# The pooling branch's output product as seven products of quarters instead of eight

## The chip, the cores and the metric

The kernel runs on one core of a Trainium2 chip. The metric is the device time of one execution in microseconds, lower is better; each figure is the median of several runs.

## The reference

One decoder block of width 1024 over 1024 positions, in float32. After a modulated norm, one projection makes q, k, v, z_a, u, z_b, m_a and m_b. A stick-breaking attention branch and a pooling branch are gated and mixed. The pooling branch is what changes:

```python
pooled = multiscale_causal_pool(u, pool_w, pool_scale)
p_b = (pooled * jax.nn.silu(z_b)) @ w_branch_b
merged = jax.nn.sigmoid(m_a) * p_a + jax.nn.sigmoid(m_b) * p_b
out = merged @ w_out
return x + gate[:, None, :] * out
```

Here (pooled * silu(z_b)) is 1024 x 1024 and w_branch_b is 1024 x 1024.

## The kernel before

**Split products.** Every float32 operand is held as two float32r tiles, a rounded one (hi) and the rest (lo = value - hi). A product a·b is three matmuls per block, hi·hi, hi·lo and lo·hi, into one PSUM bank. One matmul has a stationary block of 128 x 128 and 512 moving columns, so an output bank of 128 x 512 over an inner size of 1024 takes 24 matmuls. load_w loads a 128-column tile of a weight into `raw` (2 buffers) and splits it into `whl` (2 buffers): a cast by one engine (L123 ACT or L127 DVE), a subtraction by another (L118, DVE or POOL).

**Stages.** In order: the modulated norm and the first half of u; the second half of u (8 banks); v (16 banks, two halves of eight); z_b (wzb, 8 tiles of two banks each); the pooling product (pb, 8 tiles of two banks); then one long stage with the remaining projections (p) woven into the attention; then the branch sums (pa) and the output (o). Positions run along the free dimension, so the pooling product takes weight blocks as stationary and `gb` as moving operand: gb[j] is channel block j of pooled * silu(z_b), 128 x 1024, held as hi and lo. Each output bank is copied by ACT (L661) into `sm` and stored to pb_d, which is read much later.

**PSUM.** Eight banks in four tags of two: pj, z, av, tr. The projections and the pooling product use pj alone. ACT reads a bank (u_sg, vo, zs or sm), in v and wzb DVE too, before PE can write it again.

**Low tiles.** The lo half of 32 weight tiles of the long stage is made ahead of time by make_lo and kept in HBM (wl_d). One low tile: SP loads the tile (l_raw, L152), ACT casts it (l_hi, L155), DVE subtracts in place (L156), SP stores it (wl_d, L157). Eight are placed in u, ten in v, four in wzb, ten in pb (LO_V, LO_ZB, LO_PB). They are first read in the long stage, after its eighth weight tile.

**Order.** Outside the hand-pinned parts a scheduler decides, when the program is built, in which order each engine takes its instructions; on the chip each engine's queue and the DMA queues of SP and ACT are strictly in order, so an instruction that waits holds all behind it on its engine. A tile's buffer count (bufs) says how many uses may overlap.

Of the kernel before, what the change touches and what calls it, by code (L numbers as in the profile page):

```python
# [9 lines left out]
F32 = mybir.dt.float32  # L10
F32R = mybir.dt.float32r
# [46 lines left out]
def block_kernel(ctx, tc, a, out):  # L58
# [3 lines left out]
    def pool(name, **kw):  # L62
        return tc.tile_pool(name=name, bufs=1, reuse_waits="tile", **kw)
# [9 lines left out]
    def bank(tag, name):  # L73
        return psp.tile([P, 512], F32, tag=tag, bufs=BANKS[tag], name=name)
# [64 lines left out]
    tiles += gates  # L139
    early_lo = iter(range(PLAIN, len(tiles)))  # L140

    def make_lo(pl, n, tag=None, bufs=3, later=False):

        rest = []
        for _ in range(n):
            i = next(early_lo)
            if tag:
                raw, hi = (pl.tile([P, D], t_, tag=tag, bufs=5, name=f"l{i}_{n_}") for n_, t_ in (("raw", F32), ("hi", F32R)))
            else:
                raw = pl.tile([P, D], F32, tag="lraw", bufs=bufs, name=f"l{i}_raw")  # L150
                hi = pl.tile([P, D], F32R, tag="lhi", bufs=1, name=f"l{i}_hi")
            nc.sync.dma_start(raw, a["w_in"][tiles[i]])  # L152

            def low(i=i, raw=raw, hi=hi):
                act.copy(hi, raw)  # L155
                v.tensor_sub(raw.bitcast(F32R), raw, hi.bitcast(F32))  # L156
# [31 lines left out]
    def hmov(sh):  # L188
        return lambda m, kb: m[:, kb, sh * 512:sh * 512 + 512]
# [390 lines left out]
    with pool("vp") as vp:  # L580
        def load_wv(hf, k2):
            raw = wts.tile([P, 2, 512], F32, tag="raw", bufs=2, name=f"wv{hf}_{k2}_raw")
            nc.sync.dma_start(raw.rearrange("p k c -> p (k c)"), a["w_v"][hf, k2])
            return split(raw, [P, 2, 512], vp, "wv", 6, act, v, f"wv{hf}_{k2}")

        wv = [[load_wv(0, k2) for k2 in range(4)]]
        for i in reversed(range(KB)):
            ps = bank("pj", f"u{i}_1")
            mm3(ps, whl[i], h, range(KB), hmov(1))
            use[i](1, ps)  # L590
            make_lo(vp, 1)
        early.close()
        diffs = ExitStack()
        todo = []
        dif = diffs.enter_context(pool("dif", side="right"))
        for hf in range(2):
            if hf == 0:
                wv.append([load_wv(1, k2) for k2 in range(4)])
            for sb in range(8):
                ss = slice(sb * P, (sb + 1) * P)  # L600
                ps = bank("pj", f"v{sb}_{hf}")
                for kb in range(KB):
                    hh, hl = h_hi[:, kb, ss], h_lo[:, kb, ss]
# [6 lines left out]
                act.copy(vo[:, :, 0], pv)  # L610
                v.tensor_sub(vo[:, :, 1], pv, vo[:, :, 0].bitcast(F32))  # L611
# [12 lines left out]


    with pool("pb") as pb:
        gb = pb.tile([P, 2, KB, S], F32R, name="gb")
        for j in range(KB):
            if j not in dhls:
                make_d(j, load_u(j))  # L630
            zs = [pb.tile([P, 512], F32, tag="zs", bufs=3, name=f"zs{j}_{sh}") for sh in range(2)]

            def silu(sh, ps):
                z, sl = zs[sh], slice(sh * 512, sh * 512 + 512)
                act.activation(z, ps, AF.Sigmoid)
                v.tensor_mul(z, ps, z)
# [12 lines left out]
        gate = pb.tile([P, KB], F32, name="gate")
        bias = pb.tile([P, KB], F32, name="gbias")  # L650
        nc.sync.dma_start(bias, a["b_gate"])
        for j in range(KB):
            sm = [pb.tile([P, 512], F32, tag="zs", bufs=3, name=f"sm{j}_{sh}") for sh in range(2)]
            whl = load_w(a["w_branch_b"][j], f"wb{j}", v, gp)
            wg = wts.tile([P, D], F32, tag="raw", bufs=2, name=f"wg{j}")
            nc.sync.dma_start(wg, a["w_gate"][j])
            v.scalar_tensor_tensor(gjunk, wg, 1.0, sg, ALU.mult, ALU.mult, accum_out=gate[:, j:j + 1])
            for sh in range(2):
                ps = bank("pj", f"pb{j}_{sh}")
                mm3(ps, whl, (gb[:, 0], gb[:, 1]), range(KB), hmov(sh))  # L660
                act.copy(sm[sh], ps)  # L661
# [442 lines left out]
```

## Time and profile before

| | us |
|---|---|
| median of 3 runs | 1210.2 (1209.76 to 1210.31) |
| span of the profiled execution | 1210.3 |
| u, second half, and what goes before v | 91 to 128 |
| v | 128.4 to 216.5 |
| wzb | 216.7 to 303.7 |
| pb | 303.7 to 390.8 |
| long stage with p | 390.8 to about 1029 |

The profile counts an engine as busy while it has an instruction in work. For PE, matmuls overlap (one shows as 389 ns), so the rate is read from the length of an unbroken run divided by its count. "DMA share" is the mean busy share of the core's 16 DMA engines. "x<-y" names what an instruction writes and reads. A wait counts as idle time of the engine, put down to what ended it. The granted TensorE clock was 0.999 over the execution.

### The profile page before, as it was taken

How to read it: one execution, taken by the hardware profiler on the slowest of the kernel's cores; microseconds unless marked ns; L12 is line 12 of the kernel's file. 1: busy time of each engine (PE TensorE's matmuls, PEld its weight loads, DVE VectorE, ACT ScalarE, POOL GpSimd, SP SyncE). 2: the span in 40 equal slices, each digit the busy share in tenths (PEclk: the TensorE clock that was granted, in tenths of full speed). 3: DMA queues.
4: the chain of work that ended last, by engine and by line, in shares of the span. 5: the costliest groups of instructions: out<-in, count | busy, mean ns of one | idle time of the engine just before them, and what ended most of it. 6: DMA issues, size and time to landing. Idle time of an engine off the chain costs nothing.

```text
span 1210.3 us, 16177 instructions
## 1 busy us (share of the span) xinstructions
PE 1199.2 (99%) x5746; PEld 1002.5 (83%) x5746; DVE 756.5 (63%) x1050; ACT 531.6 (44%) x1008; POOL 187.2 (15%) x360
## 2 busy tenths in 40 slices
PE   8999999999999999999999999999999999999997
PEld 7888878888888888888888888888888888888886
DVE  5764483677510286767868677686777853785643
ACT  5564331334301255655555555655555643232211
POOL 1000000001221333212222222222221210000001
PEclk9999999999999999999999999999999999999999
DMA  9649995626847632442635325353343344975622
GB/s 358 255 171 325 328 356 207 209 87 225 309 148 120 191 91 76 124 122 86 170 109 156 113 80 153 110 157 118 102 134 101 99 131 167 353 272 170 216 67 83
DMA packets 81955, 207.14 MB, mean 171 GB/s; under 512 B 10449, under 2 KB 23889, under 8 KB 79698
## 3 DMA queue, kind: packets, MB, share of 16 engines
q1 hardware_dynamic: 73666, 191.23, 49.2%
q10 hardware_dynamic: 8208, 14.88, 3.3%
q8 instruction: 45, 0.74, 0.2%
q14 instruction: 36, 0.29, 0.1%
HBM read 138.96 MB, written 50.34 MB: 156 GB/s over the span
## 4 chain that ended last, share of the span: by engine, by line
PE 88%; DMA 5%; issue 3%; DVE 2%; ACT 1%; POOL 0%; POOLq 0%; ACTq 0%; DVEq 0%; SPq 0%
PE p L103 34%; PE pb L103 7%; PE wzb L103 7%; PE pa L103 7%; PE o L103 6%; PE z L103 6%; PE av L103 5%; PE wt L103 5%; PE v L103 4%; PE ua L103 3%; DMA wl_d<-l_raw 2%; DMA l_raw<-in_w_in 2%; PE u L103 2%; PE wm L103 1%; DVE l_raw L156 1%
## 5 line engine op out<-in xcount | busy, mean ns | idle before, releaser
L103 PE MATMUL p<-hT,w 128*128 128x512 f32 x1920 | 480.0, 391 | 0.5 <-ACT m_sg L201 0.5
L103 PEld LDWEIGHTS p<-hT,w 128*128 128x128 f32 x1920 | 355.2, 188 | 74.7 <-ACT m_sg L201 1.0
L826 DVE TENSOR_TENSOR_SCAN om<-om 128x512 f32<-128x512 f32 (+7 forms) x128 | 175.8, 1373 | 124.9 <-ACT om L819 69.4
L819 ACT ACTIVATE om<-z 128x512 f32<-128x512 f32 (+2 forms) x192 | 94.5, 492 | 155.9 <-PE z L103 133.5
L824 POOL TENSOR_SCALAR_AFFINE_SELECT om<-om 128x128 f32<-128x128 f32 x128 | 56.3, 440 | 346.5 <-ACT om L819 287.0
L846 DVE TENSOR_TENSOR wt<-wt,wt 128x512 fp32r<-128x512 f32 (+1 forms) x160 | 99.3, 621 | 16.1 <-ACT wt L845 15.5
L845 ACT CAST wt<-wt 128x512 fp32r<-128x512 f32 (+1 forms) x160 | 88.2, 551 | 48.1 <-PE wt L103 47.9
L103 PE MATMUL av<-wt,vv 128*128 128x512 f32 x320 | 106.4, 414 | 0.0
L103 DVE TENSOR_TENSOR be<-be,om 128x511 f32<-128x511 f32 (+7 forms) x128 | 95.1, 749 | 1.1 <-POOL be L824 0.7
L820 ACT ACTIVATE be<-z 128x512 f32<-128x512 f32 (+2 forms) x192 | 94.1, 490 | 0.0
L103 PE MATMUL pa<-ga,wa 128*128 128x512 f32 x384 | 89.6, 389 | 0.1
L103 PE MATMUL o<-wo,mhl 128*128 128x512 f32 (+1 forms) x408 | 89.6, 377 | 0.0
L103 PE MATMUL wt<-ident,be 128*128 128x128 f32 x576 | 89.4, 273 | 0.0
L103 PE MATMUL v<-wv,hT 128*128 128x512 f32 x384 | 87.8, 390 | 0.5 <-DVE vo L611 0.5
L103 PE MATMUL wzb<-hT,wzb 128*128 128x512 f32 x384 | 87.2, 389 | 0.0
L103 PE MATMUL pb<-gb,wb 128*128 128x512 f32 x384 | 87.2, 389 | 0.0
L103 PEld LDWEIGHTS v<-wv,hT 128*128 128x128 f32 x384 | 71.9, 188 | 16.2 <-DVE vo L611 1.4
L103 PEld LDWEIGHTS o<-wo,mhl 128*128 128x128 f32 x408 | 73.5, 188 | 14.1
L103 PEld LDWEIGHTS pa<-ga,wa 128*128 128x128 f32 x384 | 72.0, 188 | 15.4 <-DVE wa L118 0.5
L103 PEld LDWEIGHTS wzb<-hT,wzb 128*128 128x128 f32 x384 | 72.1, 188 | 14.9
L103 PEld LDWEIGHTS pb<-gb,wb 128*128 128x128 f32 x384 | 72.1, 188 | 14.9
L103 PEld LDWEIGHTS wt<-ident,be 128*128 128x128 f32 x576 | 70.2, 141 | 11.6
(130 smaller groups left out, 1364.5 us busy)
## 6 DMA issues: line engine op xcount, KB each, us to landing
w_raw<-in_w_in SPq DMA_DIRECT2D x40, 512.0 KB, 4.7
l_raw<-in_w_in SPq DMA_DIRECT2D x32, 512.0 KB, 5.2
wl_d<-l_raw SPq DMA_DIRECT2D x32, 512.0 KB, 5.7
w<-wl_d SPq DMA_DIRECT2D x32, 512.0 KB, 3.8
v_d<-vo SPq DMA_DIRECT2D x16, 512.0 KB, 5.2
vv<-v_d SPq DMA_DIRECT2D x8, 1024.0 KB, 5.3
wa_raw<-in_w_branch_a SPq DMA_DIRECT2D x16, 512.0 KB, 4.7
wa<-in_w_mod SPq DMA_DIRECT2D x7, 1024.0 KB, 6.4
```

The source lines that it names most:

```text
L103: ins = op(*args, **kw)
L156: v.tensor_sub(raw.bitcast(F32R), raw, hi.bitcast(F32))
L819: act.activation(om[:, b0:b0 + n], zp[:, :n], AF.Sigmoid, scale=-0.125)
L820: act.activation(be[:, b0:b0 + n], zp[:, :n], AF.Sigmoid, scale=0.125)
L824: gp.affine_select(out=tl[:, :P], in_=tl[:, :P], pattern=[[1, P]], compare_op=ALU.is_gt, fill=fill, base=0, channel_multiplier=-1)
L826: v.tensor_tensor_scan(om[:, :W], om[:, :W], om[:, :W], 1.0, ALU.mult, ALU.min)
L845: act.copy(wt[:, 0, :off], pt[:, :off])
L846: v.tensor_sub(wt[:, 1, :off], pt[:, :off], wt[:, 0, :off].bitcast(F32))
```

## The change

Three edits, made together.

**1. Seven products.** With output columns (weight halves m), inner halves k and position halves n, the product of 2 x 2 quarters is made by seven products of sums and differences of quarters (the form of Strassen's method with shared sums). `gb` now holds the plain float32 value, in place of hi and lo; t1 and t2 hold differences of its quarters, s2k sums of weight quarters. For each product and each half q of its inner size (256 rows each), the operands are loaded, combined on DVE and split (a_op for weights in the `whl` buffers, b_op for activations in `bhl`), and 4 output blocks x 2 inner blocks x 3 matmuls follow. All eight PSUM banks are used: p1, p6, p7 and p4 sum up in one set of four (pj, z), p5 and p3 in the other (av, tr), p2 in the first again. The results go out as copies (ACT) and additions (DVE).

**2. Low tiles.** ACT writes the negative of the cast (l_neg), a DMA issued by POOL adds the raw tile to it, and SP stores that. Raw and negative tiles have two buffers each; raw had three in u and v, and five shared ones in pb. The numbers placed in u, v and wzb stay, and LO_PB spreads its ten over seven products.

**3. Placement.** The vo tiles get a pool of their own. The gate's eight products with w_gate move from pb into the wzb loop and share the raw tiles' two buffers there. w_branch_b is passed untiled.

```diff
-LO_PB = (1, 1, 1, 1, 1, 1, 2, 2)
+LO_PB = (1, 2, 1, 2, 1, 2, 1)
...
-    def make_lo(pl, n, tag=None, bufs=3, later=False):
+    def make_lo(pl, n, bufs=2, later=False):
...
+            raw = pl.tile([P, D], F32, tag="lraw", bufs=bufs, name=f"l{i}_raw")
+            neg = pl.tile([P, D], F32R, tag="lneg", bufs=2, name=f"l{i}_neg")
             nc.sync.dma_start(raw, a["w_in"][tiles[i]])
 
-            def low(i=i, raw=raw, hi=hi):
-                act.copy(hi, raw)
-                v.tensor_sub(raw.bitcast(F32R), raw, hi.bitcast(F32))
-                nc.sync.dma_start(wl_d[i], raw)
+            def low(i=i, raw=raw, neg=neg):
+                act.mul(neg, raw, -1.0)
+                gp.dma_start(neg.bitcast(F32), raw, accum_op=ALU.add)
+                nc.sync.dma_start(wl_d[i], neg.bitcast(F32))
...
-                vo = dif.tile([P, 8, 2, HD], F32R, tag="vo", bufs=3, name=f"vo{sb}_{hf}")
+                vo = vop.tile([P, 8, 2, HD], F32R, tag="vo", bufs=3, name=f"vo{sb}_{hf}")
...
-        gb = pb.tile([P, 2, KB, S], F32R, name="gb")
+    gb = pb.tile([P, KB, S], F32, name="gb")
+    t1 = pb.tile([P, 4, 512], F32, name="t1")
+    t2 = pb.tile([P, 4, 512], F32, name="t2")
...
+    def b_op(src, name):
+        hl = pb.tile([P, 2, 2, 512], F32R, tag="bhl", bufs=3, name=name)
+        act.copy(hl[:, 0], src)
+        v.tensor_sub(hl[:, 1], src, hl[:, 0].bitcast(F32))
+        return hl
...
+    def a_op(src, name):
+        hl = wts.tile([P, 2, 2, 512], F32R, tag="whl", bufs=2, name=name)
+        act.copy(hl[:, 0], src)
+        v.tensor_sub(hl[:, 1], src, hl[:, 0].bitcast(F32))
+        return hl
...
+        if j < 4:
+            v.tensor_sub(t1[:, j], gb[:, j, 512:], gb[:, j, :512])
+        else:
+            v.tensor_sub(t2[:, j - 4], gb[:, j, 512:], t1[:, j - 4])
+            v.tensor_sub(gb[:, j - 4, 512:], gb[:, j, 512:], gb[:, j - 4, 512:])
+        make_lo(pb, LO_ZB[j])
...
+        wg = pb.tile([P, D], F32, tag="lraw", bufs=2, name=f"wg{j}")
...
-            whl = load_w(a["w_branch_b"][j], f"wb{j}", v, gp)
...
-            for sh in range(2):
-                ps = bank("pj", f"pb{j}_{sh}")
-                mm3(ps, whl, (gb[:, 0], gb[:, 1]), range(KB), hmov(sh))
-                act.copy(sm[sh], ps)
-                nc.sync.dma_start(pb_d[j][:, sh * 512:sh * 512 + 512], sm[sh])
-            make_lo(dif, LO_PB[j], "d")
...
+    def a_s1(q):
+        r, w = raw1(1, 0, q, f"a21_{q}"), raw2(1, 1, q, f"a22_{q}")
+        v.tensor_add(r, r, w)
+        w = raw2(0, 0, q, f"a11s_{q}")
+        v.tensor_sub(k2(s2k, q), r, w)
+        return r
...
+    products = (
+        ("p1", lambda q: raw1(0, 0, q, f"a11_{q}"), lambda q: part(gb, 0, 0, q)),
+        ("p5", a_s1, lambda q: k2(t1, q)),
+        ("p6", lambda q: k2(s2k, q), lambda q: k2(t2, q)),
+        ("p7", a_s3, lambda q: part(gb, 0, 1, q)),
+        ("p4", lambda q: raw1(1, 1, q, f"a22_{q}"), b_t4),
+        ("p3", a_s4, lambda q: part(gb, 1, 1, q)),
+        ("p2", lambda q: raw1(0, 1, q, f"a12_{q}"), lambda q: part(gb, 1, 0, q)),
+    )
+    ta, tb = ("pj", "pj", "z", "z"), ("av", "av", "tr", "tr")
...
+        for q in range(2):
+            wl_, ml_ = a_op(a_of(q), f"{name}a{q}"), b_op(b_of(q), f"{name}b{q}")
+            for j in range(4):
+                for e in range(2):
+                    for i, (w, m) in enumerate(((0, 0), (0, 1), (1, 0))):
+                        mm(
+                            ps[j], wl_[:, w, e, j * P:(j + 1) * P], ml_[:, m, e],
...
+            elif name == "p7":
+                out_b(j + 4, 1, added(copied("s3", 2, j, ps[j]), chain["b"][j]))
+            elif name == "p4":
+                out_b(j + 4, 0, copied("s4", 2, j, ps[j]))
...
+        make_lo(pb, LO_PB[n])
```

The changed program's order is known before it runs. On PE, before, the pooling product is a plain row of banks, 24 matmuls each, tile by tile (the name is the bank, then the operands):

```order
L103 MATMUL wzb_1_2306<-hT,wzb_2273 128x512 x24
L103 MATMUL pb_0_2360<-gb,wb_2354 128x512 x24
L103 MATMUL pb_1_2387<-gb,wb_2354 128x512 x24
L103 MATMUL pb_0_2430<-gb,wb_2424 128x512 x24
L103 MATMUL pb_1_2457<-gb,wb_2424 128x512 x24
```

Now, at the passage from the second half of product p7 to p4 (p7a and p7b are its weight and activation operands, 2639 and 2642 those of the second half; p_0 to p_3 are the four banks):

```order
L103 MATMUL p_0_2351<-p7b_2642,p7a_2639 128x512 x4
L103 MATMUL p_1_2352<-p7b_2642,p7a_2639 128x512 x4
L103 MATMUL p_2_2353<-p7b_2642,p7a_2639 128x512 x4
L103 MATMUL p_3_2354<-p7b_2642,p7a_2639 128x512 x4
L103 MATMUL p_0_2351<-p4b_2703,p4a_2699 128x512 x6
L103 MATMUL p_1_2352<-p4b_2703,p4a_2699 128x512 x6
L103 MATMUL p_0_2351<-p4b_2736,p4a_2732 128x512 x2
L103 MATMUL p_1_2352<-p4b_2736,p4a_2732 128x512 x2
L103 MATMUL p_0_2351<-p4b_2736,p4a_2732 128x512 x4
L103 MATMUL p_1_2352<-p4b_2736,p4a_2732 128x512 x4
L103 MATMUL p_2_2353<-p4b_2703,p4a_2699 128x512 x6
```

The banks are now woven: p4 takes the second half of its operands (p4a_2732) after 12 matmuls on the first half, two banks at a time.

On ACT, at the passage from u to v, before (l_hi is the cast of a low tile; nine such casts stand ahead of the first vo here, of which these rows show the last three):

```order
L155 CAST l_hi<-l_raw 128x1024
L208 COPY u_sg_1082<-u_1_1057 128x512
L209 DMA u_d<-u_sg_1082 128x512
L155 CAST l_hi<-l_raw 128x1024
L208 COPY u_sg_1116<-u_1_1091 128x512
L155 CAST l_hi<-l_raw 128x1024
L209 DMA u_d<-u_sg_1116 128x512
L610 CAST vo_0_1174<-v_0_1149 128x8x64
L155 CAST l_hi<-l_raw 128x1024 x2
L610 CAST vo_0_1206<-v_0_1181 128x8x64
```

And now (l_neg is the negation of a low tile; the one just ahead of vo_0_1177 is the seventh):

```order
L152 ACTIVATE l_neg<-l_raw 128x1024
L205 COPY u_sg_1116<-u_1_1091 128x512
L206 DMA u_d<-u_sg_1116 128x512
L152 ACTIVATE l_neg<-l_raw 128x1024
L609 CAST vo_0_1177<-v_0_1152 128x8x64
L152 ACTIVATE l_neg<-l_raw 128x1024
L609 CAST vo_0_1209<-v_0_1184 128x8x64
L609 CAST vo_0_1244<-v_0_1219 128x8x64
L152 ACTIVATE l_neg<-l_raw 128x1024
L609 CAST vo_0_1283<-v_0_1258 128x8x64
```

Two low tiles have moved from u into v, and in v they stand further apart; sixteen stores of low tiles now stand ahead of the last v_d store in SP's queue, before it was eighteen.

On ACT again, at the end of wzb, before (zs and gb belong to the wzb banks):

```order
L635 ACTIVATE zs_0_2186<-wzb_0_2193 128x512
L155 CAST l_hi<-l_raw 128x1024
L638 CAST gb<-zs_0_2186 128x512
L155 CAST l_hi<-l_raw 128x1024
L635 ACTIVATE zs_1_2187<-wzb_1_2223 128x512
L638 CAST gb<-zs_1_2187 128x512
L635 ACTIVATE zs_0_2269<-wzb_0_2276 128x512
L155 CAST l_hi<-l_raw 128x1024
```

And now (wzb_0_2107 is the eleventh of the sixteen banks, wzb_1_2305 the last; p1a are weight operands of the first product):

```order
L152 ACTIVATE l_neg<-l_raw 128x1024 x2
L663 ACTIVATE gb<-wzb_0_2107 128x512
L663 ACTIVATE gb<-wzb_1_2135 128x512
L123 CAST wzb_2274<-wzb_raw 128x1024
L152 ACTIVATE l_neg<-l_raw 128x1024 x2
L663 ACTIVATE gb<-wzb_0_2195 128x512
L663 ACTIVATE gb<-wzb_1_2223 128x512
L653 CAST p1a_2357<-a_0_2355 128x1024
L152 ACTIVATE l_neg<-l_raw 128x1024 x2
L663 ACTIVATE gb<-wzb_0_2277 128x512
L663 ACTIVATE gb<-wzb_1_2305 128x512
L653 CAST p1a_2389<-a_1_2387 128x1024
```

The negations now stand in pairs, one pair to two banks, and a fourth pair follows right behind these rows, ahead of the casts for p5. From the first p tile of the long stage on, the order of every engine is the old one.

More of the change, by code (lines that the diff above doesn't have):

```diff
@@ L667, in block_kernel, with part @@
-    diffs.close()
+        vouts.close()
+    pbs = ExitStack()
+    pb = pbs.enter_context(pool("pb"))
+    gb = pb.tile([P, KB, S], F32, name="gb")
+    t1 = pb.tile([P, 4, 512], F32, name="t1")
+    t2 = pb.tile([P, 4, 512], F32, name="t2")
+    gate = pb.tile([P, KB], F32, name="gate")
+    bias = pb.tile([P, KB], F32, name="gbias")
+    nc.sync.dma_start(bias, a["b_gate"])
+    sg = pb.tile([P, D], F32, name="sg")
+    def part(src, k, n, q):
+        return src[:, 4 * k + 2 * q:4 * k + 2 * q + 2, 512 * n:512 * n + 512]
@@ new lines, in b_op, with load_a @@
+    def b_op(src, name):
[3 more added lines that the diff above has]
+        return hl
+    def load_a(m, k, q, pl, tag, name):
+        raw = pl.tile([P, 2, 512], F32, tag=tag, bufs=2, name=name)
+        r0 = (4 * k + 2 * q) * P
+        nc.sync.dma_start(raw, a["w_branch_b"][r0:r0 + 2 * P, 512 * m:512 * m + 512].rearrange("(k p) c -> p k c", p=P))
+        return raw
+    def a_op(src, name):
[3 more added lines that the diff above has]
+        return hl
@@ new lines, in block_kernel, with silu @@
+    for j in range(KB):
+        if j not in dhls:
+            make_d(j, load_u(j))
+        def silu(sh, ps):
+            z = gb[:, j, sh * 512:sh * 512 + 512]
+            act.activation(z, ps, AF.Sigmoid)
+            v.tensor_mul(z, ps, z)
+            v.scalar_tensor_tensor(z, dhls[j][:, sh * 512:sh * 512 + 512], psc_v[:, j:j + 1], z, ALU.mult, ALU.mult)
+        project(CZB + j, f"wzb{j}", silu, act, v)
+        if j < 4:
[4 more added lines that the diff above has]
+        make_lo(pb, LO_ZB[j])
+        if j == 0:
+            nc.sync.dma_start(sg, a["c_row"].broadcast_to([P, D]))
+            gjunk = pb.tile([P, D], F32, tag="lraw", bufs=2, name="gjunk")
+            act.activation(gjunk, sg, AF.Sigmoid)
+            v.tensor_mul(sg, sg, gjunk)
+        wg = pb.tile([P, D], F32, tag="lraw", bufs=2, name=f"wg{j}")
+        nc.sync.dma_start(wg, a["w_gate"][j])
+        v.scalar_tensor_tensor(wg, wg, 1.0, sg, ALU.mult, ALU.mult, accum_out=gate[:, j:j + 1])
+        del dhls[j]
@@ new lines, in block_kernel, with raw1, raw2, k2 @@
+    v.tensor_add(gate, gate, bias)
+    nc.sync.dma_start(g_d[0].rearrange("(k p) -> p k", p=P), gate)
+    diffs.close()
+    sums = pbs.enter_context(pool("sums", side="right"))
+    s2k = sums.tile([P, 4, 512], F32, name="s2k")
+    def raw1(m, k, q, name):
+        return load_a(m, k, q, wts, "raw", name)
+    def raw2(m, k, q, name):
+        return load_a(m, k, q, sums, "ar", name)
+    def k2(t, q):
+        return t[:, 2 * q:2 * q + 2]
+    def a_s1(q):
[4 more added lines that the diff above has]
+        return r
@@ new lines, in block_kernel, with out_b, copied, added @@
+    ta, tb = ("pj", "pj", "z", "z"), ("av", "av", "tr", "tr")
+    chain = {}
+    keep = {}
+    def out_b(j, n, t):
+        nc.sync.dma_start(pb_d[j][:, 512 * n:512 * n + 512], t)
+    def copied(tag, bufs, j, src):
+        t = sums.tile([P, 512], F32, tag=tag, bufs=bufs, name=f"{tag}_{j}")
+        act.copy(t, src)
+        return t
+    def added(t, src):
+        v.tensor_add(t, src, t)
+        return t
+    for n, (name, a_of, b_of) in enumerate(products):
+        c = {"p5": "b", "p3": "b", "p2": "c"}.get(name, "a")
+        if c not in chain:
+            chain[c] = [bank((tb if c == "b" else ta)[j], f"{name}_{j}") for j in range(4)]
+        ps = chain[c]
+        for q in range(2):
[5 more added lines that the diff above has]
+                            ps[j], wl_[:, w, e, j * P:(j + 1) * P], ml_[:, m, e],
+                            start=name in ("p1", "p5", "p2") and (q, e, i) == (0, 0, 0), stop=(q, e, i) == (1, 1, 2),
+                                skip_group_check=True,
+                        )
+        for j in range(4):
+            if name == "p1":
+                keep["s1", j] = copied("s1", 4, j, ps[j])
+            elif name == "p6":
+                keep["s2", j] = copied("s2", 4, j, ps[j])
+            elif name == "p7":
+                out_b(j + 4, 1, added(copied("s3", 2, j, ps[j]), chain["b"][j]))
+            elif name == "p4":
+                out_b(j + 4, 0, copied("s4", 2, j, ps[j]))
+            elif name == "p3":
+                out_b(j, 1, added(keep["s2", j], ps[j]))
+            elif name == "p2":
+                out_b(j, 0, added(keep["s1", j], ps[j]))
+        make_lo(pb, LO_PB[n])
@@ L670, in block_kernel @@
+    pbs.close()
     logits = ExitStack()
```

49 lines of the change are left out of this document (14 added, 35 removed).

## The prediction

> **What bounds the kernel now.** I read the page first: busy times, then the chain that ended last.
>
> ```profile
> PE 1199.2 (99%) x5746; PEld 1002.5 (83%) x5746; DVE 756.5 (63%) x1050; ACT 531.6 (44%) x1008; POOL 187.2 (15%) x360
> PE 88%; DMA 5%; issue 3%; DVE 2%; ACT 1%; POOL 0%; POOLq 0%; ACTq 0%; DVEq 0%; SPq 0%
> ```
>
> TensorE is busy for 99% of the span and carries 88% of the chain. A busy PE need not be useful, so the next view is the chain in order of time (start, length, what):
>
> ```profile
> 216.69 87.04 PE wzb L103 x384
> 303.73 87.04 PE pb L103 x384
> 390.77 25.16 PE p L103 x111
> ```
>
> The two stages around the change, the z_b projection (wzb) and the pooling product (pb), are unbroken runs of 384 matmuls at 87.04 / 384 = 0.2267 us each. One PSUM bank of 24 matmuls takes 5.44 us. While PE runs like this, everything else is free only as long as it stays ahead. The table by stage shows how far ahead (stretch, length, then PE, PEld, DVE, ACT, POOL busy, PE clock, DMA share, GB/s):
>
> ```profile
> 91.00:128.00 37.00, 37.00 (x164) 30.31 (x163) 14.42 (x13) 15.25 (x19) 0.00 (x0) 1.00 0.90 313
> 128.00:216.50 88.50, 87.97 (x387) 72.22 (x386) 49.10 (x66) 23.54 (x31) 0.00 (x0) 1.00 0.83 293
> 216.50:303.50 87.00, 87.00 (x385) 72.07 (x384) 64.06 (x81) 33.87 (x47) 3.27 (x1) 1.00 0.51 172
> 303.50:390.60 87.10, 87.10 (x386) 72.13 (x385) 23.20 (x31) 16.04 (x23) 19.13 (x8) 1.00 0.69 197
> ```
>
> In the u and v stages (91 to 216.5) the scarce thing beside PE is the DMA engines, at 0.90 and 0.83. In wzb it is DVE, 64 of 87 us. In pb nothing is scarce. PE waited there hardly at all:
>
> ```profile
> PE v L103 <- DVE vo L611: 0.5, 2, 0.3
> ```
>
> But the low tiles already run just in time. The chain between 90 and 180 us passes through them:
>
> ```profile
> 95.41 1.06 ACT l_hi L155
> 96.49 1.24 DVE l_raw L156
> 97.74 5.66 DMA wl_d<-l_raw
> 103.47 9.17 DMA l_raw<-in_w_in
> ```
>
> Cast, subtraction, store and next load follow each other in one buffer, 17 us a turn here, with three buffers. And ACT, which must empty the PSUM banks, stands behind them:
>
> ```profile
> 124.62 1.05 ACT L155 CAST l_hi<-l_raw 128x1024 fp32r<-128x1024 f32 x1 [5.79 <-DMA l_raw<-in_w_in]
> 125.57 0.58 ACT L208 COPY u_sg<-u 128x512 f32<-128x512 f32 x1
> ```
>
> ACT idled 5.79 us for a load, and a finished bank of u waited behind it. With two banks, PE stops only if a copy is later than 5.44 - 0.59 = 4.85 us. So there is a margin, and it was partly used.
>
> **What goes: matmuls.** Eight products of quarters become seven. Each is 4 column blocks x 4 row blocks x 3 = 48 matmuls, so 384 become 336. I take the same 0.2267 us each: all have one loaded 128x128 block against 512 columns, and the wzb run, which loads as often, has that rate. 48 x 0.2267 = **-10.9 us**, all on PE and all on the chain. Nothing else in this change shortens the chain, so 1210.3 - 10.9 = 1199.4 is the floor. From the first p tile on, each engine's new order is the old one, so no term lies behind 391 us.
>
> **What comes: operand work.** Each of 28 operand halves (14 weight, 14 activation) needs a cast on ACT and a subtraction on DVE; ten more subtractions or additions of 1024 columns form the combinations, and 28 copies and additions read PSUM. The prices:
>
> ```profile
> L118 DVE TENSOR_TENSOR wzb<-wzb_raw,wzb 128x1024 fp32r<-128x1024 f32 x6 | 7.3, 1217 | 0.0
> L636 DVE TENSOR_TENSOR zs<-wzb,zs 128x512 f32<-128x512 f32 x15 | 10.3, 687 | 10.4 <-ACT zs L635 10.4
> L661 ACT COPY sm<-pb 128x512 f32<-128x512 f32 x16 | 9.4, 588 | 59.1 <-PE pb L103 59.1
> L123 ACT CAST w<-w_raw 128x1024 fp32r<-128x1024 f32 x2 | 2.1, 1052 | 0.0
> L118 POOL TENSOR_TENSOR w<-w_raw,w 128x1024 fp32r<-128x1024 f32 x2 | 4.8, 2392 | 17.8 <-ACT w L123 17.8
> ```
>
> DVE: 38 x 1.217 + 12 x 0.687 = 54.5 us. ACT: 28 x 1.052 + 16 x 0.588 = 38.9, with ten negations at 1.05 49.4. Both lie beside 336 x 0.2267 = 76.2 us of PE, and the first few are made during wzb. The worst product, p5, asks 8 x 1.217 = 9.7 us of DVE in its 10.9. So on average it is hidden, at little margin. In wzb DVE loses about 9 subtractions of low tiles (11.0) and 16 of gb (11), and gains 12 differences (8.2), six gate products (7.3) and six operand splits (7.3): 64 becomes about 65 of 87. Cost nothing, with 20 us of cover.
>
> The product stage has edges, though. A weight buffer of a block is free only when the block two before has finished, and then cast and subtraction take 1.05 + 1.22 = 2.3 us of a block's 5.44. In p4 the order lets PE reach the second block after 12 matmuls, 2.7 us, so there 0.4 us is left. At the end, the first p tile takes its buffer 5.44 us before the last product ends and needs 1.05 + 2.39 = 3.4 us: it fits. I cost these edges at **+1 us**. Below stands nothing; above, a late load at each of the last six blocks at about a microsecond, 6 us.
>
> **What is moved: the low tiles.** The subtraction leaves DVE; ACT now writes the negative cast, and a DMA from POOL's queue adds the raw tile to it. The trace has no DMA that adds. Its time X, issue to landing, has these nearest rows:
>
> ```profile
> q<-qlo SPq DMA_DIRECT2D x32, 128.0 KB, 2.4
> vv<-v_d SPq DMA_DIRECT2D x8, 1024.0 KB, 5.3
> wa<-in_w_mod SPq DMA_DIRECT2D x7, 1024.0 KB, 6.4
> wa<-in_w_mod SPq DMA_DIRECT2D x2, 512.0 KB, 10.2
> ```
>
> The lower end is 2.4 (SBUF to SBUF, a quarter of the size), the upper 10.2 (the right size, at the start, when the engines were full). The addition must fetch both tiles, 1024 KB, so I take the 1024 KB rows: 5.3 where the engines are half idle, 6.4 where they are full. The Trainium skill, "DMA: Bandwidth & Descriptors", section "Anatomy of one DMA — SWDGE (gpsimd) path", fits a DMA from this queue as 2.0 us + bytes / 436e3, which gives an estimate of 3.2 us for one tile; by it X would cost nothing anywhere and the sum would be 1200.4. No run here shows that fit yet. "Collectives: The Full Stack", section "The bandwidth ceiling: the fold count and why AG ≠ RS ≠ AR", says that an adding DMA is slow because it reads two sources, not because of the addition; that would make it 4.4 us, still under what I take.
>
> Now the turn of a buffer. The load of the tile after next waits for X, with two buffers each for raw and negative: turn = landing + negation + X. Landings:
>
> ```profile
> l_raw<-in_w_in SPq DMA_DIRECT2D x17, 512.0 KB, 6.5
> wl_d<-l_raw SPq DMA_DIRECT2D x18, 512.0 KB, 6.8
> l_raw<-in_w_in SPq DMA_DIRECT2D x10, 512.0 KB, 4.9
> ```
>
> (The first two are of 80 to 200 us, the last of 230 to 335.) The order of ACT gives the deadlines. The first negation can stand where the first cast stood, and the seventh, three turns later, stands ahead of the first vo copy:
>
> ```profile
> 90.67 1.05 ACT L155 CAST l_hi<-l_raw 128x1024 fp32r<-128x1024 f32 x1
> 133.99 0.59 ACT L610 CAST vo<-v 128x512 fp32r<-128x512 f32 x1 [2.60 <-PE v L103]
> ```
>
> It may start at 133.99 + 4.85 - 1.05 = 137.8 at the latest: three turns in 47.1, 15.7 us a turn. With the median landing a turn is 6.5 + 1.05 + 6.4 = 14.0, which fits. But the additions make the engines fuller, so I take the longest landing seen, 9.17: 16.6, which is 0.9 over in each of three turns, **+3 us** (2.8). Ends: nothing at X = 2.4; at X = 10.2, 20.4 a turn, 3 x 4.7 = 14 us.
>
> In wzb, pairs of negations stand between the ACTIVATEs that empty its banks. The first pair follows unit 10, which ends at 216.69 + 54.4 = 271.1; the fourth stands ahead of the cast for p5, needed by about 303.7 + 10.9 - 2.3 = 312. After 0.6 of ACTIVATE and 2.1 for the last pair, three turns in 38.2 us: 12.7 each. A turn costs 4.9 + 2.1 + 5.3 = 12.3: **0**, by 0.4 us. At X = 10.2 it is 17.2, 3 x 4.5 = 14 us; below, nothing. SP matters here too: its queue is in order, and behind each store of a low tile, which waits for the addition, stand v_d stores, wzb loads and the loads of p5. They slip by the same lag as ACT, not once more. On POOL the additions have only each other behind them until the first p tile; the eight subtractions of weight blocks (2.4 us and more each) are gone from it.
>
> **Sum.** 1210.3 - 10.9 + 1 + 2.8 + 0 = 1203.2 by the profiled execution, whose span is 0.1 above the median of the runs. I give **1203.3 us**.
>
> **Rivals.**
>
> 1. *The additions overfill the DMA engines in u and v, and it ends slower.* The engines are busy 0.90 x 37 + 0.83 x 88.5 = 106.8 of 125.5 us there, 18.7 free. Two tiles move out of the stretch: 4 transfers at 0.524 MB / 350 GB/s (313 / 0.90) = 1.5 us, 6 us. With PE's margin of 4.85 that is 29.6 us for 16 additions: it decides from 1.85 us of engine time each. One pass of 0.5 MB is 1.5, two reads are 3.0. At 3.0, 16 x 1.15 = 18.4 us come back, through v_d stores and vo buffers, as waits of v: 1210.3 - 10.9 + 18.4 + 1 = 1218.8, and 1224 with the edges at their upper end. For it: the shares. Against: shares count packets that overlap, and the PE waits of 0.5 us show that a share near 1 did not yet stop v.
> 2. *The seven products are fed late.* p5 leaves DVE 1.2 us, and its six loads stand in SP's queue behind the stores. The DMA engines had 0.69 x 87.1 = 60 us of work in this stage; ten more weight loads of 1.5 add 15, eight gate loads (12) leave, and some eight additions add 12 to 24: 75 to 87 in 76 us. If p5 and every late block slip, the 6 us bound and 2 to 3 us at p5 add up: about 1208 to 1210, nearly all of the gain gone.
> 3. *Nothing of the low tiles reaches PE:* X is short, and DVE, which no longer stands in their chain, frees vo sooner. Then 1199.4 plus at most the edges: 1199.4 to 1200.4.
>
> **Chances.** Forecast, 1200.5 to 1207.8: 0.39. Rival 3: 0.21, and 0.02 for less than 1198.5. Rival 2 with what lands within 0.2% (2.4 us, about what a measurement of this kernel can tell from no change): 0.14. Rival 1: 0.24, of which 0.08 lie above 1224 if X is at its upper end in both stages. That makes faster 0.62, same 0.14, slower 0.24; the range 1198.5 to 1224 leaves out 0.1, since the unknown X alone spans from nothing to 28 us.
>
> **What would show it.** Right: 336 matmuls in the product stage at 0.227 us; PE waits between 91 and 135 us of a few us, ended by ACT copies of u or v; the adding DMA at 5 to 7 us; the p stage starting about 7 us earlier, and the same length from there. Wrong: PE idle before p5 or p4 (rival 2); v_d stores landing late, with PE waits spread over v at a DMA share near 1 (rival 1); landings as before and X under 4 (rival 3). Matmuls slower than 0.2267 in the seven products would break the first term.

## The result, and the profile after

| | before | after |
|---|---|---|
| median of the runs, us | 1210.2 (1209.76 to 1210.31) | 1246.74 (1242.94 to 1247.53) |
| span of the profiled execution, us | 1210.3 | 1244.4 |
| ratio after / before | | 1.0291, 95% interval 1.0274 to 1.0309 |

One further run of before took 4418 us and is left out. The kernel became 36.5 us slower. The prediction (1203.3, range 1198.5 to 1224.0) was wrong in sign and size. The page of the changed kernel, busy times and the shares of the chain:

```profile
PE 1205.1 (97%) x5698; PEld 1000.4 (80%) x5698; DVE 760.4 (61%) x1056; ACT 548.5 (44%) x1020; POOL 196.8 (16%) x384
...
PE 73%; DMA 18%; issue 4%; ACT 2%; DVE 1%; SPq 1%; POOL 0%; POOLq 0%; ACTq 0%; DVEq 0%
```

PE has 48 matmuls fewer and is busy 5.9 us longer, and its part of the chain fell from 88% to 73%, while that of the DMAs rose from 5% to 18%. The waits of PE (what it was about to do, who released it, total, times, longest):

```profile
PE wzb L103 <- DVE gb L664: 15.9, 7, 3.6
PE v L103 <- DVE vo L610: 6.0, 2, 3.2
PE p L103 <- ACT p5a L653: 5.7, 2, 3.2
```

The same by stage, u, v, z_b and the seven products (stretch, length, then PE, PEld, DVE, ACT, POOL busy, PE clock, DMA share, GB/s):

```profile
91.00:130.40 39.40, 39.40 (x174) 32.28 (x173) 8.06 (x9) 14.94 (x19) 4.59 (x5) 1.00 0.91 284
130.40:225.60 95.20, 89.25 (x386) 73.08 (x385) 37.10 (x53) 23.95 (x31) 9.63 (x11) 0.98 1.03 319
225.60:339.20 113.60, 97.70 (x385) 77.69 (x385) 61.10 (x85) 31.27 (x39) 10.50 (x12) 0.91 0.87 250
339.20:424.00 84.80, 79.07 (x337) 63.78 (x336) 49.76 (x49) 37.89 (x46) 5.92 (x5) 0.98 0.76 239
```

Against the boundaries of before, v begins 2.0 us late, v lasts 6.9 us longer and z_b 26.6 us longer; the product is only 2.3 us shorter. What follows lasts 0.9 us longer. The sum is the 34.1 us by which the span grew.

Two things make up z_b's 26.6: PE waits 15.9 us, and its matmuls are busy 97.7 us where before they took 87.0, at a granted clock of 0.91. The second part comes along with the first: in v and z_b of before, where PE hardly waited, the clock was 1.00.

The chain in v shows what the DMAs are (start, length, what):

```profile
145.21 1.07 ACT l_neg L152
146.28 0.35 issue
146.63 8.19 DMA l_neg<-l_raw
...
154.84 0.74 SPq L154
...
155.62 9.11 DMA l_raw<-in_w_in
...
164.83 1.06 ACT l_neg L152
```

This is the turn of a low tile's buffer: negation, addition, load of the next tile, 19.6 us (145.21 to 164.83), of which the adding DMA is 8.2 and the load 9.1. In z_b ACT waits for this loop with the banks of PE behind it. A group of ACT and one of VectorE from 225.6 to 339.2 (busy, mean ns, idle time before them and its releasers):

```profile
L152 ACT ACTIVATE l_neg<-l_raw 128x1024 fp32r<-128x1024 f32 x12 | 12.7, 1059 | 67.3 <-DMA l_raw<-in_w_in 61.5 <-issue 5.8
...
L664 DVE TENSOR_TENSOR gb<-wzb,gb 128x512 f32<-128x512 f32 x15 | 10.2, 687 | 29.1 <-ACT gb L663 29.1
```

ACT waited 61.5 us for loads of low tiles there, in a queue that is in order, with the ACTIVATEs of z_b's banks (gb, L663) next in it. VectorE's step L664, which released PE in the waits above, waited 29.1 us for them.

### The profile page after: what moved, and what is told of

It is laid out like the page before. It is cut to its first block, busy times and chain, and to the rows that moved or that the text cites. A ratio compares the mean times of both kernels' runs of the same rounds, so it can differ in the third digit from the quotient of the medians.

```text
span 1244.4 us, 16180 instructions
## 1 busy us (share of the span) xinstructions
PE 1205.1 (97%) x5698; PEld 1000.4 (80%) x5698; DVE 760.4 (61%) x1056; ACT 548.5 (44%) x1020; POOL 196.8 (16%) x384
## 4 chain that ended last, share of the span: by engine, by line
PE 73%; DMA 18%; issue 4%; ACT 2%; DVE 1%; SPq 1%; POOL 0%; POOLq 0%; ACTq 0%; DVEq 0%
PE p L103 38%; DMA l_raw<-in_w_in 7%; DMA l_neg<-l_raw 7%; PE pa L103 7%; PE o L103 6%; PE z L103 5%; PE av L103 5%; PE wt L103 5%; PE u L103 3%; PE ua L103 3%; DMA a<-in_w_branch_b 1%; ACT l_neg L152 1%; DMA wa<-in_w_mod 1%; DMA u_d<-u_sg 1%; DMA wt<-in_w_ut 1%
## 5 line engine op out<-in xcount | busy, mean ns | idle before, releaser
L103 PE MATMUL wzb<-hT,wzb 128*128 128x512 f32 x384 | 97.8, 418 | 15.9 <-DVE gb L664 15.9
L103 PEld LDWEIGHTS wzb<-hT,wzb 128*128 128x128 f32 x384 | 77.7, 204 | 35.9 <-DVE gb L664 18.9
L103 PEld LDWEIGHTS v<-wv,hT 128*128 128x128 f32 x384 | 73.0, 191 | 22.1 <-DVE vo L610 6.8
L152 ACT ACTIVATE l_neg<-l_raw 128x1024 fp32r<-128x1024 f32 x32 | 33.8, 1059 | 127.5 <-DMA l_raw<-in_w_in 121.7
L153 POOL DMA_DIRECT2D l_neg<-l_raw x32 | 28.2, 886 | 277.7 <-ACT l_neg L152 213.4
```

The costliest lines, as they stand in the source:

```text
L103: ins = op(*args, **kw)
L152: act.mul(neg, raw, -1.0)
L153: gp.dma_start(neg.bitcast(F32), raw, accum_op=ALU.add)
```

## The experiments

Two theories after the result. **A:** the adding DMAs cost the kernel, as load on the DMA engines. **B:** the rest of the change (products, placement of side work) costs too. All times are medians; the runs of before beside them had medians of 1210.6 to 1211.4. The twelve runs in one table; the last columns, from the profiled execution, are where v and z_b begin and where the last matmul of the pooling product starts:

| run | us | ratio to before | v from | z_b from | last of product |
|---|---|---|---|---|---|
| before | 1210.3 | | 128.4 | 216.5 | 390.4 |
| after | 1246.7 | 1.0291 | 130.5 | 225.7 | 423.9 |
| e1, subtraction on VectorE | 1217.1 | 1.0053 | 131.0 | 218.1 | 395.4 |
| e4, subtraction on GpSimd | 1221.4 | 1.0084 | 130.4 | 222.8 | 402.0 |
| e5, plain DMA copy | 1220.8 | 1.0079 | 130.0 | 217.1 | 399.6 |
| e6, e1 with two more stores | 1244.1 | 1.0264 | 129.7 | 222.7 | 421.2 |
| e2, before with additions in u, v | 1229.4 | 1.0148 | 129.7 | 221.5 | 405.4 |
| f5, low tiles as before | 1213.9 | 1.0021 | 129.1 | 216.1 | 393.7 |
| f1, f5 with gates' own buffer | 1219.4 | 1.0069 | 128.5 | 216.5 | 399.4 |
| f3, after with gates' own buffer | 1242.9 | 1.0262 | 129.9 | 223.1 | 419.2 |
| h1, f5 with all side work held back | 1213.6 | 1.0017 | 128.1 | 216.4 | 388.5 |
| h3, after with all side work held back | 1269.2 | 1.0489 | 130.3 | 222.4 | 408.1 |
| h4, f5 with low tiles held back | 1203.6 | 0.9942 | 128.2 | 215.2 | 381.5 |
| h5, h4 with gates' own buffer | 1206.0 | 0.9956 | 128.1 | 215.7 | 384.7 |

### The addition alone

**e1.** The changed kernel, but VectorE makes the low part:

```diff
-                act.mul(neg, raw, -1.0)
-                gp.dma_start(neg.bitcast(F32), raw, accum_op=ALU.add)
+                act.copy(neg, raw)
+                v.tensor_sub(neg, raw, neg.bitcast(F32))
```

> The changed kernel with one edit: the low tile is made by a cast on ACT and a subtraction on DVE into the same tile, so the adding DMA is gone and the two buffers each stay. Theory (the new way of making low tiles costs it all, the seven products keep their 10.9 us less some edges): 1200 to 1205 us, PE waits in v and wzb under 2 us together, wzb back at about 87 us. Rival (the seven products and the moved gate work cost it): 1230 us or more, with the waits of PE in wzb still there.

Measured: 1217.08 (ratio 1.0053, 1.0037 to 1.0070). The additions cost 29.7 of the 36.5 us, but what is left is no gain: theory A is not all. The time lies between the two ranges expected, 1200 to 1205 and 1230 or more, so neither came true as a whole.

**e4.** The same subtraction on GpSimd:

```diff
-                act.mul(neg, raw, -1.0)
-                gp.dma_start(neg.bitcast(F32), raw, accum_op=ALU.add)
+                act.copy(neg, raw)
+                gp.tensor_tensor(neg, raw, neg.bitcast(F32), op=ALU.subtract)
```

> The changed kernel with one edit: cast on ACT and subtraction on POOL in place of the adding DMA. If it is the DMA engines' time for the addition that counts, or the length of its turn (7.3 us against some 3 on POOL), both go: 1200 to 1206 us. If POOL and DVE hold each other up, as the POOL subtraction beside L637 suggested in the profile of before (2456 ns against 752), DVE instructions get longer in wzb and PE waits there: 1206 to 1215 us.

Measured: 1221.36 (ratio 1.0084, 1.0068 to 1.0100). 25.4 us better than the DMA, but above both ranges expected. The subtraction takes 2.56 us there, and GpSimd is busy 74 us with 29 of them from 91 to 320. What the second theory named is seen, VectorE's instructions get longer; here its step L665 in z_b, in the changed kernel and in e4:

```profile
L665 DVE SCALAR_TENSOR_TENSOR gb<-d,vecs,gb 128x512 f32<-128x512 f32 x15 | 11.1, 748 | 0.2
L665 DVE SCALAR_TENSOR_TENSOR gb<-d,vecs,gb 128x512 f32<-128x512 f32 x15 | 17.4, 1161 | 0.3
```

Whether that makes the 4.3 us to e1 was not tested.

**e5.** A plain copy in place of the addition, by the same queue, with the same waits. The low part of the 32 weight tiles is left out.

```diff
-                gp.dma_start(neg.bitcast(F32), raw, accum_op=ALU.add)
+                gp.dma_start(neg.bitcast(F32), raw)
```

> The changed kernel with one edit: POOL's DMA copies the raw tile without adding, so each low tile holds the raw tile itself and the low parts of 32 weights are left out of the result's precision. If the second read is what makes the addition dear, the engine time of one falls from 2.8 us to about 1.4 and its landing from 7.3 to about 5: 1218 to 1230 us. If what counts is that a transfer stands in the chain at all: 1240 us or more, the same landing. If it costs nothing more than a subtraction would: 1200 to 1206.

Measured: 1220.77 (ratio 1.0079, 1.0064 to 1.0094), 26.0 us better than with the addition, and v is an unbroken 87 us again. The step in the buffer's turn and GpSimd's queue are the same here, so most of the price is what the addition does beyond a copy. Step and copy aren't free: e5 stays 3.7 us above e1, its z_b still lasts 104 us (114 with the addition), and between 216 and 340 ACT still waits 56 us for loads of low tiles (65 in the changed kernel). The DMA queues of the changed kernel between 91 and 226 us, u and v (queue: packets, MB, share of 16 engines; then issues: count, KB, median us to landing):

```profile
q1 hardware_dynamic: 14356, 31.42, 63.6%
q0 software_dynamic: 2190, 7.99, 30.9%
...
l_neg<-l_raw POOLq DMA_DIRECT2D x16, 512.0 KB, 7.4
...
v_d<-vo SPq DMA_DIRECT2D x15, 512.0 KB, 8.8
l_raw<-in_w_in SPq DMA_DIRECT2D x14, 512.0 KB, 8.0
```

q0 holds the DMAs that POOL issues, here the additions alone. And of the plain copy, same stretch:

```profile
q1 hardware_dynamic: 15468, 34.05, 72.5%
q0 software_dynamic: 2334, 8.51, 16.4%
...
l_neg<-l_raw POOLq DMA_DIRECT2D x17, 512.0 KB, 6.2
```

For almost the same bytes the adding queue holds the engines 30.9% of 135 us, 41.7 us; at 7.99 / 0.524 = 15.2 tiles that is 2.74 us of all 16 engines each. The copy takes 16.4%, 22.1 us for 16.2 tiles, 1.36 each. An addition costs the engines two copies, as far as these shares tell: they count packets that overlap (the share of v above is 1.03). Its landing, 7.4 against 6.2, hardly shows that.

**e6.** If load is the price, load without anyone waiting for its result must cost as much. e1 with each low tile stored twice more to an area that nobody reads:

```diff
                 nc.sync.dma_start(wl_d[i], neg.bitcast(F32))
+                for n in range(2):
+                    nc.sync.dma_start(xt_d[i, n], neg.bitcast(F32))
```

> The subtraction on VectorE as in the run before (1217.1), and two more stores of each low tile to a scratch area that nobody reads: about 3 us more of all DMA engines a tile, as much as an addition, with no one who waits for its landing but the buffer's next use. If the additions cost engine capacity: 1235 us or more. If they cost only as a step that the turn of a buffer waits for: up to 1223.

Measured: 1244.09 (ratio 1.0264, 1.0249 to 1.0279), 27.0 above e1. Its v_d stores land in 10.4 us. These stores also hold the negative tile's buffer longer, so load and turn aren't wholly apart here. Nor is the loss in the same place: 16.9 us of PE's waits are for p5 (5.7 in the changed kernel), whose loads stand in SP's queue among these stores. So the near equality with the 29.7 us of the additions shows little; that load costs time is what e6 and e5 have in common.

**e2.** The addition alone in the kernel before, in u and v, with two raw and two cast tiles:

```diff
-                raw = pl.tile([P, D], F32, tag="lraw", bufs=bufs, name=f"l{i}_raw")
-                hi = pl.tile([P, D], F32R, tag="lhi", bufs=1, name=f"l{i}_hi")
+                add = bufs == 3
+                raw = pl.tile([P, D], F32, tag="lraw", bufs=2, name=f"l{i}_raw")
+                hi = pl.tile([P, D], F32R, tag="lhi", bufs=2 if add else 1, name=f"l{i}_hi")
...
+                if not tag and bufs == 3:
+                    act.mul(hi, raw, -1.0)
+                    gp.dma_start(hi.bitcast(F32), raw, accum_op=ALU.add)
+                    nc.sync.dma_start(wl_d[i], hi.bitcast(F32))
+                    return
```

> The kernel before with one edit: in u and v alone the low tiles are made by negation and the adding DMA, two buffers each; wzb and the old pooling product as before. Theory (low tiles): the loss of the changed kernel up to the start of wzb comes here too, 2 us in u and 7 in v, and nothing more: 1217 to 1221 us. Rival (the seven products or the moved gate work): 1210 to 1212 us.

Measured: 1229.35 (ratio 1.0148, 1.0133 to 1.0163), 18.2 us slower than the runs beside it, more than the 1217 to 1221 expected. Where the waits show, in z_b and in v (engine and line, released by, total, times, longest):

```profile
PE wzb L103 <- DVE zs L642: 6.0, 3, 4.1
PE v L103 <- DVE vo L617: 2.4, 1, 2.4
```

Most of it is seen in z_b, where no more than the last of v's additions still run: z_b lasts 97 us in place of 87, v 92 in place of 88. The lag of v's low tiles arrives a stage later. The edit also takes away one of three raw buffers, so the 18.2 us are not the additions' alone; but e1 and e5, with two buffers as well, have an unbroken v.

### The rest of the loss

**f5.** The changed kernel with low tiles in the form of before (three raw buffers in u and v, subtraction in place), the gates as changed:

```diff
-            neg = pl.tile([P, D], F32R, tag="lneg", bufs=2, name=f"l{i}_neg")
+            hi = pl.tile([P, D], F32R, tag="lhi", bufs=1, name=f"l{i}_hi")
...
-                act.mul(neg, raw, -1.0)
-                gp.dma_start(neg.bitcast(F32), raw, accum_op=ALU.add)
-                nc.sync.dma_start(wl_d[i], neg.bitcast(F32))
+                act.copy(hi, raw)
+                v.tensor_sub(raw.bitcast(F32R), raw, hi.bitcast(F32))
+                nc.sync.dma_start(wl_d[i], raw)
...
-            make_lo(vp, 1)
+            make_lo(vp, 1, bufs=3)
```

> As the run beside it (seven products, low tiles as before the change), but the gate loads stay in the z_b stage and in the ring of the low tiles' two raw buffers. Theory that the shared ring holds ACT and VectorE there: 1207 to 1213 us, with PE waiting in z_b for the gb steps of VectorE. Rival (the ring is harmless, the negation form alone was at fault): 1200 to 1204.

Measured: 1213.86 (ratio 1.0021, 1.0013 to 1.0030), just above the first theory's range; PE waits 2.6 us for gb steps, but more elsewhere. v is as before; z_b still lasts 92 us, and PE waits 6.3 us ahead of p5. The chain there:

```profile
304.96 7.17 DMA wl_d<-l_raw
312.15 0.33 SPq L149
...
312.57 5.53 DMA wl_d<-l_raw
318.12 0.33 SPq L149
...
318.50 4.84 DMA a<-in_w_branch_b
```

The weights of p5 stand in SP's queue behind loads of low tiles (L149) that wait for one of two buffers, each released only by a store.

**f1 and f3.** Gate products at the end of each product, with a buffer of their own, in f5 (f1) and in the changed kernel (f3, where two output copies share a pair of buffers to make room):

```diff
-        wg = pb.tile([P, D], F32, tag="lraw", bufs=2, name=f"wg{j}")
-        nc.sync.dma_start(wg, a["w_gate"][j])
-        v.scalar_tensor_tensor(wg, wg, 1.0, sg, ALU.mult, ALU.mult, accum_out=gate[:, j:j + 1])
...
+        for j in range(n, n + 1 + n // 6):
+            wg = pb.tile([P, D], F32, tag="wg", bufs=1, name=f"wg{j}")
+            nc.sync.dma_start(wg, a["w_gate"][j])
+            v.scalar_tensor_tensor(wg, wg, 1.0, sg, ALU.mult, ALU.mult, accum_out=gate[:, j:j + 1])
```

> The seven products as changed, but the low tiles made as before the change (subtraction on VectorE inside the raw tile, three raw buffers in u and v), and the eight gate products back in the product stage with a buffer of their own. Theory: nothing is left of the change but the seven products, so the z_b stage is an unbroken 87 us again and the time is 1200 to 1204 us. Rival (the seven products themselves, or the operands made early in z_b, cost the rest): 1208 to 1213, with waits left in z_b or ahead of p5.

> The changed kernel with its adding DMAs, but the gate products moved to the product stage with a buffer of their own. Theory that the additions are the larger part by themselves: 1230 to 1238 us (some 10 less than the changed kernel). Rival, that addition and shared ring only hurt together: 1210 to 1217.

Measured: f1 1219.36 (ratio 1.0069, 1.0053 to 1.0085), f3 1242.93 (1.0262, 1.0248 to 1.0277). Both expectations missed, because the edit didn't move the work. VectorE's groups of f1 in z_b, 216.5 to 322.5:

```profile
L153 DVE TENSOR_TENSOR l_raw<-l_raw,l_hi 128x1024 fp32r<-128x1024 f32 x14 | 17.1, 1220 | 19.4 <-ACT l_hi L152 19.4
...
L772 DVE SCALAR_TENSOR_TENSOR wg<-wg,sg 128x1024 f32<-128x1024 f32 x8 | 9.7, 1218 | 1.8 <-DMA wg<-in_w_gate 1.7
```

All eight gate products still ran in z_b, and with the shared ring relieved 14 low tiles came forward too, where f5 had 9: what has its inputs and a buffer is scheduled early, wherever it stands in the code. f1 showed something else: with nothing late, the seven products run unbroken.

```profile
L103 PE MATMUL p<-p1b,p1a x48: 388/392/398, 322.7 to 333.5; 128*128 128x512 f32 x48
...
L103 PE MATMUL p<-p2b,p2a x48: 388/392/394, 388.7 to 399.4; 128*128 128x512 f32 x48
```

From 322.7 to 399.6 they take 76.9 us, 0.229 each, against 87.0 for the eight products of before.

**h1 and h3.** In h1 and h3 the side work was tied to buffers that exist only in the product stage: the cast tile of the ten low tiles, and the gate loads from the fourth product on, in f5 (h1) and in the changed kernel (h3, with one buffer for the negative tile there and the output copies sharing theirs).

```diff
+            hi = (hp or pl).tile([P, D], F32R, tag="lhi", bufs=1, name=f"l{i}_hi")
...
-        make_lo(pb, LO_PB[n])
+        make_lo(pb, LO_PB[n], hp=sums)
+        for j in range(2 * n - 6, 2 * n - 4) if n > 2 else ():
+            wg = sums.tile([P, 2, 512], F32, tag="ar", bufs=2, name=f"wg{j}").rearrange("p k c -> p (k c)")
...
```

> Seven products; low tiles made as before the change; and the side work held back to the product stage, where it stood before: the cast tiles of the ten low tiles that belong there, and the eight gate loads from the fourth product on, come from buffers that exist only in that stage, so VectorE has 4 low tiles and no gate product in z_b in place of 9 to 14 low tiles and 8 gate products. Theory that what was left (1213.9 us) is VectorE's and ACT's side work pulled forward into z_b, and the two-buffer ring that the loads for p5 stand behind: z_b an unbroken 87 us, 1200 to 1204 us. Rival, that the operand work of the products itself (differences and splits in z_b) is too much there: PE waits of some us in z_b remain, 1207 to 1214.

> The changed kernel with its adding DMAs, and the side work held back to the product stage as in the run beside it (one buffer for the negative tile there). Theory that the additions fill the DMA engines in u and v, and that the lag is carried into z_b, whatever is placed there: 1222 to 1232 us. Rival, that the additions cost only because more low tiles were pulled into z_b: 1205 to 1212.

Measured: h1 1213.59 (ratio 1.0017, 1.0004 to 1.0029; its runs spread from 1209.8 to 1217.1; the profiled one took 1210.7). Half of the expectation came: z_b is an unbroken run again. But the loss moved. z_b and the products of h1, by stretch:

```profile
216.00:304.00 88.00, 88.00 (x390) 72.89 (x389) 56.48 (x72) 24.61 (x32) 0.00 (x0) 1.00 0.39 132
304.00:392.00 88.00, 82.38 (x350) 66.20 (x349) 70.28 (x77) 44.55 (x53) 3.66 (x2) 0.98 0.90 291
```

The DMA share is 0.39 in z_b and 0.90 in the products, where p4 and p2 wait for DMAs that land late. Their pieces of the chain:

```profile
350.97 6.08 DMA pb_d<-s
...
369.53 12.38 DMA a<-in_w_branch_b
```

An output copy of p4 waits for a store that frees its buffer, and p2 for its weights, 12.4 us on the way.

h3 took 1269.21 (ratio 1.0489, 1.0474 to 1.0503), outside both expectations. The additions, crowded behind the products, held SP's queue until the long stage stood still. PE waited 33.9 us there, in two waits:

```profile
PE p L103 <- DVE klo L103: 33.9, 2, 24.6
```

**h4 and h5.** The low tiles of the product stage held back as in h1, the gates left in z_b as changed (h4); and with one buffer of their own there, paid for by sharing two output copies' buffers (h5).

```diff
-        make_lo(pb, LO_PB[n])
+        make_lo(pb, LO_PB[n], hp=sums)
```

> Seven products, low tiles made as before the change, the ten low tiles of the product stage held back there, but the eight gate products left in z_b, in the ring of the low tiles' two buffers. Theory, that what is left is a matter of spreading side work over two stages: z_b has VectorE at about 56 + 10 of 87 us, the product stage about 60 of 77 and 8 loads fewer (DMA share 0.90 less some 0.14), so both are unbroken: 1200 to 1204 us. Rival, that the shared ring holds VectorE in z_b or the loads of p5 by itself: 1206 to 1212 with waits there.

> As the run beside it, but the gate loads of z_b have one buffer of their own, and two output copies of the products share one pair of buffers to make room. If the shared ring matters, this is faster than the run beside it by some us and ends at 1200 to 1204; if not, the two are equal within 2 us.

Measured: h4 1203.60 (1203.34 to 1204.15), ratio 0.9942 (0.9928 to 0.9955): **0.6% faster than before**, and in the range expected. h5 took 1206.04, ratio 0.9956 (0.9944 to 0.9969): 2.4 us more than h4, outside both of its expectations. Its z_b is 2.1 us longer, so relieving the ring gained nothing here; why it cost something was not followed. The four stages of h4:

```profile
91.00:128.00 37.00, 37.00 (x164) 30.27 (x163) 14.71 (x13) 15.42 (x19) 0.00 (x0) 1.00 0.95 330
128.00:216.00 88.00, 88.00 (x390) 72.88 (x389) 49.12 (x66) 24.43 (x31) 0.00 (x0) 1.00 0.79 285
216.00:304.00 88.00, 87.75 (x387) 72.27 (x386) 65.60 (x90) 24.61 (x33) 0.00 (x0) 1.00 0.54 180
304.00:384.00 80.00, 78.78 (x343) 63.83 (x343) 60.85 (x60) 44.16 (x52) 3.40 (x2) 1.00 0.79 270
```

All are nearly unbroken at a clock of 1.00, and neither DMA nor VectorE is full in z_b or the products.

So the way from after to h4 is 43.1 us: 29.7 for the additions (after to e1), 3.2 for the old form of the low tiles with three buffers (e1 to f5), and 10.3 for holding ten of them back (f5 to h4). These parts hold for this order of steps: holding back with the additions still in (h3) made the kernel slower by 22.5 us.

## Why the prediction was wrong, point by point

**The matmuls: right.** 336 matmuls, 10.1 us saved where nothing is late (f1), 10.9 forecast; each took 0.229 in place of 0.2267 us. That h4 ends at 1203.6, beside the 1203.3 forecast, is luck: it has no additions and other placements, so other terms make up its sum.

**Operand work: the sum right, the place wrong.** For VectorE in z_b "about 65 of 87" was forecast, and the changed kernel has 61.1 us. But the forecast took each stage's work to stay in its stage. The scheduler brought forward what had a buffer: of low tiles there are 12 in z_b here (four placed there), 9 before, 14 in f1. In f5, which has 9 as well, this cost 10.3 us with the averages far from full: h4 differs from it in nothing else.

**The edges of the products: too small.** Forecast +1, at most 6. The stage took 84.8 us in place of 76.9: +7.9, 5.7 of it PE's waits for p5, whose loads stood behind the low tiles, as the second rival had it.

**The turn in u and v: right up to its deadline.** Forecast: three turns of 16.6 us, and PE 2.8 us late at the first vo copy. The first negation began at 92.88 and the seventh at 142.44, three turns of 16.5 us in the mean, and PE waited 3.2 us there. Behind this deadline the forecast had none: the next turns are longer, 19.6 us in the one shown, and PE waited another 2.8 us in v. The stretch to the end of v became 8.9 us longer, inside the bounds of 0 to 14, with 2.0 us of it from before v, whose cause is open. X was taken as 6.4 and measured 7.4 in the median, 8.2 in the turn shown; the loads slowed down with it, to 8.0. The Trainium skill, "DMA: Bandwidth & Descriptors", section "Anatomy of one DMA — SWDGE (gpsimd) path", fits such a DMA as 2.0 us + bytes / 436e3, an estimate of 3.2 us for one tile. No addition of the changed kernel landed that fast: the median was 7.4 in u and v, the shortest of all 4.5.

**The turn in z_b: the step that failed.** Forecast 0, at most 14; z_b took 26.6 us more. The price of a turn was off by less. The second negations of the last pairs began at 307.08, 323.25 and 336.01, so the turns took 16.2 and 12.8 us, 12.3 forecast. The landings from 226 to 339 were close to the 4.9 and 5.3 forecast, though the engines were at 0.87 and not half idle (0.51 before):

```profile
l_raw<-in_w_in SPq DMA_DIRECT2D x12, 512.0 KB, 5.5
l_neg<-l_raw POOLq DMA_DIRECT2D x12, 512.0 KB, 5.3
```

What was wrong in the main is which turns count. The forecast counted three, from the pair of negations behind the tenth bank on, as if that pair came on time and nothing before it could hold PE. PE's timeline shows a wait behind every second of the sixteen banks:

| PE waited ahead of bank | 3 | 5 | 7 | 9 | 11 | 13 | 15 |
|---|---|---|---|---|---|---|---|
| us | 3.55 | 1.94 | 1.36 | 1.51 | 1.14 | 3.05 | 3.36 |
| the 48 matmuls behind the wait, us | 13.78 | 12.81 | 11.22 | 11.18 | 11.17 | 12.80 | 13.80 |

Only the last two waits, 6.4 us, stand behind the pairs that were counted. The first five, 9.5 us, come earlier, where six single negations stand in ACT's queue. Four of them end behind such negations; the one ahead of bank 5 ends behind the load of sg, which stood in SP's queue behind a low tile's store. Two of the six negations are left over from v: they ran at 232.40 and 236.35, ahead of the ACTIVATE of z_b's first bank at 238.25. Of this lag the forecast carried nothing into z_b; e2 agrees, where additions in u and v alone made z_b 10 us longer. And a wait of PE was priced at its length, while the matmuls behind the longer waits ran at a lower granted clock: 10.7 of the 26.6 us.

**The first rival: right in kind, and too low in chance.** It named 3.0 us of engine time for an addition; 2.74 was measured, well over its point of decision, 1.85. It named 18.4 us for the additions of u and v, and e2 measured 18.2, but that is close by luck: the rival looked for waits in v, while e2 lost most in z_b and had one raw buffer less. Its total of 1218.8 was short because it left z_b's additions and placement at nothing. What spoke for it stood in the prediction: two reads for each addition, and a DMA share of 0.83 to 0.90. The Trainium skill, "Collectives: The Full Stack", section "The bandwidth ceiling: the fold count and why AG ≠ RS ≠ AR", says that the add is slower because it needs two source reads; the traces agree, with 2.74 us in the changed kernel against 1.36 in e5. The forecast used the two reads for a landing time only, and not as load on engines that were nearly full.

## What to carry to other kernels

Where a stage's DMA share is near 0.9, price a new DMA by the engine time that it adds, against what is free, before its landing: halving that load (e5) gave back 26 us, while the step in the chain stayed. Count every instruction that stands ahead of a bank's copy in an engine's queue, from the first bank of the stage on, with what the stage before left over. Buffers decide when side work runs: give work that belongs to a later stage a buffer that exists only there, and look at each stage's share of DMA and of the helping engines after that. When two stages trade side work, the sum is unchanged and the time isn't: h4 and h1 hold the same work, 10 us apart.

## What was not expected of the hardware

An adding DMA from SBUF to SBUF of 512 KB took 2.74 us of all 16 DMA engines (from shares that count overlapping packets), twice a plain copy of the same size and queue (1.36), while its landing was only a fifth longer (7.4 against 6.2 us).

In z_b of the changed kernel, where PE was made to wait, the granted clock fell to 0.91, and to 0.78 in its last 14 us; single matmuls took up to 796 ns in place of 389:

```profile
L103 PE MATMUL wzb<-hT,wzb x384: 387/389/796, 225.7 to 339.0; 128*128 128x512 f32 x192
...
325.00:339.20 14.20, 13.63 (x48) 11.02 (x49) 6.40 (x9) 3.81 (x5) 2.27 (x3) 0.78 1.00 273
```

Not every wait went with that. In the table of z_b above, the 48 matmuls behind the waits of 1.1 to 1.5 us took 11.2 us, against 11.0 in the first 48 with no wait ahead; those behind waits of 1.9 to 3.6 us took 12.8 to 13.8. In v a wait of 3.2 us had no such effect (16.6 us for the next 72 matmuls, as before the change). In h4, with hardly a wait, the clock stayed at 1.00. That waits lower the clock is seen only from their going together; no run tried it apart.

Open stays why the kernels with two raw buffers begin v 1.3 to 2.6 us later than before, while f1, h1, h4 and h5 with three don't (f5, with three, begins it 0.7 us later).
